# Order of ScalarE and VectorE work in the first Strassen pair: S1 split amid pair two's scalings, unit a ahead of S4, t2 amid the weight sums, row squares at the end

## The chip, the cores and the metric

The kernel runs on one core of one Trainium2 chip. The metric is device time in microseconds, the median of several executions. One more execution is recorded by the hardware profiler; from it come the page and the trace. The engines are named as in the profile: PE is TensorE's matmul, PEld its weight load, DVE is VectorE, ACT is ScalarE, SP is SyncE (here it only starts loads and stores).

## The reference, cut to what matters

One layer: RMS norm, a projection of 1056 tokens from 1024 to 3072 channels, two mixers (a gated short convolution and a pooling), an output projection, a residual and a final RMS norm.

```python
def _rmsnorm(x, g):
    r = lax.rsqrt(jnp.mean(xf * xf, axis=-1, keepdims=True) + EPS)
    return (xf * r).astype(x.dtype) * g

proj = jnp.einsum('bsd,de->bse', h, w_in)               # h: normalised x
b_g, c_g, u, z_a, v, z_b = jnp.split(proj, ...)
cu = c_g * u                                            # conv input
y_a = b_g * conv3(cu) * jax.nn.silu(z_a)
pooled = causal_window_mean(v) - v                      # windows 2, 4, 8, 16
y_b = (pooled @ pool_w) * pool_scale * jax.nn.silu(z_b)
y = concat(y_a, y_b) @ w_out ;  out = _rmsnorm(x + y, final_g)
```

All data is float32. The kernel computes a product of float32 numbers with three passes of a shorter format: each operand is split into a high half (ScalarE copies it) and a low half (VectorE subtracts the copy from the source), and high x low, low x high and high x high are added up. The norm's weight is folded into the projection weights, and its factor per token is applied to the products afterwards.

## The kernel before, in words

The tokens stand in three column blocks of 352 (n0, n1, n2; TN = 352), the channels in eight blocks of 128. The 24 output tiles of the projection are computed in twelve pairs. Pair zero is a plain product that runs while x arrives. Every later pair p computes its two tiles over n0 and n1 with one step of a Strassen-Winograd scheme, and over n2 plainly.

- The token side of the scheme is made once: A11, A12, A22, A21 and S1 to S4, each split into halves. S1f, S2f, S3f and S4f are the unsplit sums.
- The weight side is made for each pair. load_w(p) starts a load of 1 MB on SP into the buffer "tw", gain_w(p) scales it by the norm's weight on ScalarE (eight operations, L210), make_t(p) takes sums of it on VectorE (step 0 is L218, step 1 is L220 and L221), and make_unit(p, "a") to "d" splits raw weights (a, b) or sums (c, d) into units. The high half is ScalarE's at L158, the low half VectorE's at L159. In the profile the units are wa, wb, wc, wd.
- block(bank, p, name, x, ...) issues twelve matmuls of one unit half against one token block (L245). The blocks of a pair run in this order: B11 into bank a, T2 into b, T1 into c, the plain n2 product l, B21 into a, T3 into b, the plain product r, T4 into b, B22 into c. Pair one has its own order: l, B11, r, B21, T2, T1, T3, (B11 of pair two), T4, B22.
- VectorE reads the banks on the way: t1 = b + s1 must be taken before T3 adds to b, t2 = b + s1 before T4 adds to b. s1 is ScalarE's copy of bank a after B11.

Beside the pairs the kernel gets the norm's factor. For rows 0 to 639 square_rows(t, xk) on ScalarE squares a tile of 128 rows and sums it (L256); its tiles xk are loaded into R, R2 and up, and load_rows refills R and R2 for tiles three and four after their first squares. For the rest of the tokens squares_last and squares_head make squares earlier, and sums_last and sums_head (VectorE, L267 to L285) add them into acc. In pair two, hook "rest" lets TensorE sum acc over channels (L292), ScalarE copies that out (L293, L294), and rows() makes the factor in a chain of small operations of both engines (L300 to L310) and two diagonal matrices (L314 on ScalarE, L315 on VectorE), which six matmuls pr (L322) spread over the partitions. The hook "early" of pair two then loads, scales and sums pair three's weights.

What sets the order: up to the end of pair one, PE, ACT, DVE and POOL keep the order in which the code is written (`tc.manual_schedule(engines={ET.PE, ET.Activation, ET.DVE, ET.Pool})`). From pair two on, only PE does; a scheduler orders the others by its own estimates. SP's loads start in order, each when its buffer is free. The last reader of pair two's raw weights is the low half of unit b of pair two (L159); then pair three's load can start.

Of the kernel before, what the change touches and what calls it, by code (L numbers as in the profile page):

```python
# [15 lines left out]
KD = D // P  # L16
KH = KD // 2
# [45 lines left out]
def trunk(ctx, tc, xt, xres, xct, w_first, w_in, w_out, pool_w, par, fg, sconv, spool,  # L63
# [13 lines left out]
    MUL, ADD, SUB = ALU.mult, ALU.add, ALU.subtract  # L77
    n0, n1, n2 = cols
    vt = nc.vector.tensor_tensor

    def tmp(name, dtype=F32):
        return tp.tile([P, TOK], dtype, tag="tmp", name=name)
# [7 lines left out]
    def xtile(tag, name):  # L90
        return xp.tile([P, 2, KH, TN], F32R, tag=tag, name=name)
# [26 lines left out]
    def load_w(p):  # L118
        t = wp.tile([P, 4, KH * P], F32, tag="tw", name=f"wraw_{p}")
        nc.sync.dma_start(t, w_in[:, 2 * p - 2:2 * p].rearrange("p t (h k) c -> p (t h) (k c)", h=2))  # L120
        wraw[p] = t
# [34 lines left out]
    def split2(hi, lo, src):  # L156

        nc.scalar.activation(hi, src, AF.Copy)  # L158
        nc.vector.tensor_tensor(lo, src, hi.bitcast(F32), op=ALU.subtract)  # L159

    def split(dst, src):
        split2(dst[:, 0], dst[:, 1], src)
# [7 lines left out]
    def split_x(n, k, m):  # L170
        dst = blocks[n, k // KH]
        ks = slice(k % KH, k % KH + m)
        split2(dst[:, 0, ks], dst[:, 1, ks], raw[n][:, k:k + m])


    def wtile(i, shape, name, dtype=F32R):
        return wp.tile(shape, dtype, tag=f"wt{i}", name=name)
# [3 lines left out]
    def prep_w0(k):  # L181
        t, q = w0[k // KH], k % KH
        src, g = wfraw[:, k, :2 * P], wfraw[:, k, 2 * P:]
        nc.scalar.activation(t[:, 0, q], src, AF.Copy, scale=g)
        nc.vector.scalar_tensor_tensor(t[:, 1, q], src, g, t[:, 0, q].bitcast(F32),
                                       op0=ALU.mult, op1=ALU.subtract)
# [3 lines left out]
    def project_first(n, k):  # L190
        if k == 0:
            for i in range(2):
                pm[i, n] = bank(f"pm_{i}_{n}")[:, :TN]
        for s, (a, b) in enumerate(((0, 0), (1, 0), (0, 1))):
            for i in range(2):
                nc.tensor.matmul(pm[i, n], w0[k // KH][:, a, k % KH, i * P:(i + 1) * P],  # L196
                                 blocks[n, k // KH][:, b, k % KH],
                                 start=k == 0 and s == 0, stop=k == KD - 1 and s == 2)
# [4 lines left out]
    unit = {}  # L203
    tw = {}

    def gain_w(p):
        for k in range(KD):
            t = wraw[p][:, 0::2] if k < KH else wraw[p][:, 1::2]
            t = t[:, :, k % KH * P:(k % KH + 1) * P]
            nc.scalar.activation(t, t, AF.Copy, scale=gain[:, k:k + 1])  # L210

    def make_t(p, steps=(0, 1)):
        w = wraw[p]
        if 0 in steps:
            tw[p] = wp.tile([P, 4, KH * P], F32, tag="wraw", name=f"tw_{p}")
        t = tw[p]
        if 0 in steps:
            vt(t[:, 0:2], w[:, 2:4], w[:, 0::2], op=SUB)  # L218
        if 1 in steps:
            vt(t[:, 2], w[:, 3], t[:, 0], op=SUB)  # L220
            vt(t[:, 3], w[:, 1], t[:, 2], op=SUB)  # L221
# [3 lines left out]
    def make_unit(p, u):  # L225
        if p not in slot:

            q = slot[p - 1]
            slot[p] = {"a": q["spare"], "d": q["a"], "c": q["c"], "b": q["d"], "spare": q["b"]}
        t = wtile(slot[p][u], [P, 2, 2, KH * P], f"w{u}_{p}")  # L230
        src = {"a": wraw, "b": wraw, "c": tw, "d": tw}[u][p][:, 0:2 if u in "ac" else 4][:, -2:]
        split(t, src)
        unit[p, u] = t
# [17 lines left out]
    def load_rows(t, xk):  # L251
        nc.sync.dma_start(xk, xres[t * P:(t + 1) * P])
        return xk

    def square_rows(t, xk):
        nc.scalar.activation(xk, xk, AF.Square, accum_out=ss[:, t:t + 1])  # L256
# [4 lines left out]
    def squares_head(acc):  # L261
        sh = vb[:, PM:PM + KD * REST].rearrange("p (k c) -> p k c", k=KD)
        nc.scalar.activation(sh, raw[1][:, :, TN - REST:], AF.Square)
        return sh
# [6 lines left out]
    def squares_last():  # L271
        sq = []
        for k in range(0, KD, 3):
            t = tmp(f"sq_{k}").rearrange("p (k c) -> p k c", c=TN)[:, :min(3, KD - k)]
            nc.scalar.activation(t, raw[2][:, k:min(k + 3, KD)], AF.Square)
            sq.append(t)
        return sq
# [231 lines left out]
    with tc.manual_schedule(engines={ET.PE, ET.Activation, ET.DVE, ET.Pool}):  # L509
        for k in range(KD):  # L510
            prep_w0(k)
            for n in (2, 0):
                split_x(n, k, 1)
                project_first(n, k)
        nc.vector.tensor_copy(gain.rearrange("p (k o) -> p k o", o=1), wfraw[:, :, 2 * P:])
        nc.sync.dma_start(part, par)
        xk = [load_rows(t, q[:, :D]) for t, q in enumerate((R, R2, up[:, 2:]))]
        slot[1] = {"a": 2, "b": 3, "d": 4, "c": 0}
        slot[2] = {"a": 1, "d": 2, "c": 0, "b": 4, "spare": 3}
        acc = tmp("acc")  # L520
        for k in range(0, KD, 2):
            split_x(1, k, 2)
        for k in range(KD):
            project_first(1, k)
        sh = squares_head(acc)

        S3f, S2f, S1f = raw[1][:, :KH], raw[1][:, KH:], raw[0][:, :KH]
        vt(S3f, raw[0][:, :KH], raw[1][:, :KH], op=SUB)
        vt(S2f, raw[1][:, KH:], S3f, op=SUB)
        vt(S1f, raw[0][:, :KH], S2f, op=ADD)  # L530
        gain_w(1)
        make_unit(1, "a")
        make_t(1)
        make_unit(1, "b")
        load_w(2)
        for n in (2, 0):
            for i in range(2):
                nc.scalar.copy(heads[i][:, cols[n]], pm[i, n])
        sq = squares_last()
        make_unit(1, "d")  # L540
        S4f = [tp.tile([P, 2, TN], F32, tag="tmp", name=f"S4f_{h}") for h in range(2)]
        for h in range(2):
            ks = slice(2 * h, 2 * h + 2)
            vt(S4f[h], raw[0][:, KH:][:, ks], S2f[:, ks], op=SUB)
        S2 = xtile("xa", "S2")
        split(S2, S2f)
        S3 = xtile("xb", "S3")
        split(S3, S3f)


        t_0, um = tmp("t_0"), up[:, 2:]

        def plain1(i):
            pt = bank(f"lr{i}_1")[:, :TN]
            block(pt, 1, ("B11", "B12")[i], pl[0], True, False)
            block(pt, 1, ("B21", "B22")[i], pl[1], False, True)
            return pt

        pL = plain1(0)
        pa, pb, pc = (bank(f"{q}_1")[:, :TN] for q in "abc")  # L560
        s1, t1, t2 = t_0[:, n1], um[:, n0], um[:, n1]
        block(pa, 1, "B11", A11, True, False)
        nc.scalar.copy(s1, pa)
        make_unit(1, "c")
        square_rows(2, xk[2])
        gain_w(2)
        S1 = xtile("xc", "S1")
        split(S1, S1f)
        pR = plain1(1)
        block(pa, 1, "B21", A12, False, True)  # L570
        block(pb, 1, "T2", S2, True, False)
        vt(t1, pb, s1, op=ADD)
        S4 = xtile("xd", "S4")
        for h in range(2):
            ks = slice(2 * h, 2 * h + 2)
            split2(S4[:, 0, ks], S4[:, 1, ks], S4f[h])
        make_unit(2, "a")
        make_t(2)
        for i in range(2):
            nc.scalar.copy(heads[i][:, n1], pm[i, 1])  # L580
        block(pc, 1, "T1", S1, True, False)
        nc.scalar.copy(t_0[:, n2], pL)
        nc.scalar.copy(t_0[:, n0], pa)
        for t in range(2):
            square_rows(t, xk[t])
        xk += [load_rows(t, xk[t - 3]) for t in (3, 4)]
        block(pb, 1, "T3", S3, False, False)
        vt(t2, pb, s1, op=ADD)  # L588
        make_unit(2, "d")
        vt(um[:, n1], pc, t2, op=ADD)  # L590
        first_a(2)
        block(pb, 1, "T4", A22, False, True)
        vt(t_0[:, n1], pb, s1, op=ADD)
        make_unit(2, "c")
        block(pc, 1, "B22", S4, False, True)
        vt(um[:, n0], pc, t1, op=ADD)
        for t in (3, 4):
            square_rows(t, xk[t])
        for _ in sums_last(acc, sq):
            pass  # L600
        sums_head(acc, sh)
        make_unit(2, "b")
        vt(up[:, 2 + 2 * TN:], pR, t_0[:, n2], op=MUL)
        vt(up[:, 2:2 + 2 * TN], um[:, both], t_0[:, both], op=MUL)
    diag = []
# [276 lines left out]
```

## Time and profile before

| | |
|---|---|
| median of three runs | 376.91 us (376.59 to 377.08) |
| the profiled execution's time | 376.85 us |
| its span, first to last instruction | 375.1 us |
| mean granted TensorE clock | 0.995 |
| ACT busy, share of the span | 178.6 us, 48% |
| pair one, TensorE's first T2 to pair two's l | 41.03 to 58.67 us |

A timeline row has the start in us, the length in us, the engine, the line, the operation, output <- inputs, partitions and elements, and how many instructions were merged; in brackets stands the idle time ahead of it and what ended that. The length of a merged row reaches to the end of its last instruction, so neighbours can overlap: the time from start to start is what an engine needs. A row of waits has the total in us, how often, and the longest. A row of loads ends with the size and the time from issue to landing.

### The profile page before, as it was taken

Reading aid. Unit: us, or ns where it says so; the run is one execution under the profiler, and the core shown is the slowest. Engines: PE = TensorE matmul, PEld = TensorE weight load, DVE = VectorE, ACT = ScalarE, POOL = GpSimd, SP = SyncE. Lnnn points to the kernel's source line nnn. Section 1 sums busy time; section 2 is a strip of 40 time slices with the busy share of each in tenths; the row PEclk is TensorE's granted clock in tenths of the full one; section 3 lists DMA queues with packets and bytes.
Section 4 is the critical chain, followed back from the end, with each engine's and each line's share of the span. In section 5 each row is a group of like instructions: output and inputs, shape, how many; then the busy total and the mean of one; then the engine's idle time right before and its main releaser. Section 6 shows DMA issues by size and latency. Waiting matters only on the chain.

```text
span 375.1 us, 5275 instructions
## 1 busy us (share of the span) xinstructions
PE 365.2 (97%) x2114; PEld 350.1 (93%) x2114; DVE 275.4 (73%) x425; ACT 178.6 (48%) x313; POOL 1.4 (0%) x7
## 2 busy tenths in 40 slices
PE   9999999999999999999999999999999999999993
PEld 6999889999989999999999999999988889999883
DVE  4799688699999787677798776887289537222593
ACT  5799881949453453626354451731088124111212
POOL 0000000000000000000000000000000000000000
PEclk9999999999999999999999999999999999999998
DMA  7973033021041305012030511305549904000042
GB/s 205 418 265 112 3 112 114 0 85 57 2 170 59 114 0 196 34 28 86 2 112 0 204 56 33 136 6 191 210 144 381 416 32 168 4 0 2 0 182 112
DMA packets 13512, 41.68 MB, mean 111 GB/s; under 512 B 3760, under 2 KB 5040, under 8 KB 12080
## 3 DMA queue, kind: packets, MB, share of 16 engines
q1 hardware_dynamic: 13344, 41.02, 29.8%
q8 instruction: 16, 0.26, 0.3%
q10 hardware_dynamic: 144, 0.33, 0.2%
q14 instruction: 8, 0.07, 0.1%
HBM read 32.92 MB, written 8.42 MB: 110 GB/s over the span
## 4 chain that ended last, share of the span: by engine, by line
PE 78%; DVE 12%; ACT 4%; issue 2%; DMA 2%; SPq 1%; DVEq 0%; ACTq 0%
PE po L712 15%; PE b L245 13%; PE pc L782 10%; PE c L245 9%; PE r L245 8%; PE l L245 8%; PE a L245 8%; PE pm L196 5%; ACT wraw L210 2%; DMA raw<-in_xt_dram 2%; PE pp L399 1%; PE lr L245 1%; DVE yc L416 1%; DVE tw L218 1%; DVE wa L159 1%
## 5 line engine op out<-in xcount | busy, mean ns | idle before, releaser
L712 PE MATMUL po<-wo,mix 128*128 128x512 f32 (+1 forms) x264 | 56.5, 374 | 0.0
L712 PEld LDWEIGHTS po<-wo,mix 128*128 128x128 f32 x264 | 46.2, 188 | 9.7 <-DVE mix L159 0.2
L245 PE MATMUL a<-A,wa 128*128 128x352 f32 x264 | 46.4, 324 | 0.0
L245 PEld LDWEIGHTS a<-A,wa 128*128 128x128 f32 x264 | 43.3, 188 | 0.0
L210 ACT ACTIVATE wraw<-wraw,gain 128x256 f32<-128x256 f32 x88 | 36.8, 499 | 10.0 <-DMA wraw<-in_w_in_dram 10.0
L245 PE MATMUL r<-pl,wb 128*128 128x352 f32 x240 | 40.4, 324 | 0.0
L245 PE MATMUL l<-pl,wa 128*128 128x352 f32 x240 | 40.4, 324 | 0.0
L245 PEld LDWEIGHTS l<-pl,wa 128*128 128x128 f32 x240 | 39.1, 188 | 0.0
L245 PEld LDWEIGHTS r<-pl,wb 128*128 128x128 f32 x240 | 39.1, 188 | 0.0
L782 PE MATMUL pc<-mix,wo 128*128 128x416 f32 x192 | 36.5, 351 | 0.0
L782 PEld LDWEIGHTS pc<-mix,wo 128*128 128x128 f32 x192 | 35.9, 188 | 0.5
L245 PE MATMUL c<-S,wc 128*128 128x352 f32 x132 | 23.2, 324 | 0.9 <-DVE S L159 0.9
L245 PE MATMUL b<-A,wd 128*128 128x352 f32 x132 | 23.3, 325 | 0.7 <-DVE up L588 0.7
L245 PE MATMUL b<-S,wc 128*128 128x352 f32 x132 | 23.2, 324 | 0.7 <-DVE t L459 0.7
L245 PE MATMUL b<-S,wd 128*128 128x352 f32 x132 | 23.5, 324 | 0.1
L245 PE MATMUL c<-S,wb 128*128 128x352 f32 x132 | 23.1, 324 | 0.0
L245 PEld LDWEIGHTS b<-A,wd 128*128 128x128 f32 x132 | 21.6, 188 | 1.3 <-DVE up L588 0.9
L245 PEld LDWEIGHTS c<-S,wc 128*128 128x128 f32 x132 | 21.6, 188 | 1.2 <-DVE S L159 1.2
L245 PEld LDWEIGHTS b<-S,wc 128*128 128x128 f32 x132 | 21.6, 188 | 1.0 <-DVE t L459 1.0
L245 PEld LDWEIGHTS b<-S,wd 128*128 128x128 f32 x132 | 21.7, 188 | 0.4 <-DVE wd L159 0.4
L245 PEld LDWEIGHTS c<-S,wb 128*128 128x128 f32 x132 | 21.7, 188 | 0.0
L218 DVE TENSOR_TENSOR tw<-wraw 128x1024 f32<-128x1024 f32 x11 | 13.5, 1226 | 10.5 <-ACT wraw L210 10.5
(197 smaller groups left out, 528.1 us busy)
## 6 DMA issues: line engine op xcount, KB each, us to landing
wraw<-in_w_in_dram SPq DMA_DIRECT2D x11, 1024.0 KB, 4.6
woraw<-in_w_out_dram SPq DMA_DIRECT2D x8, 512.0 KB, 5.7
zt<-in_xres_dram SPq DMA_DIRECT2D x5, 512.0 KB, 6.4
spill_b<-yb SPq DMA_DIRECT2D x4, 528.0 KB, 3.5
mixraw<-spill_b SPq DMA_DIRECT2D x4, 528.0 KB, 5.8
R<-in_xres_dram SPq DMA_DIRECT2D x4, 512.0 KB, 7.9
out_yt_dram<-zt SPq DMA_DIRECT2D x4, 512.0 KB, 2.6
zc<-in_xct_dram SPq DMA_DIRECT2D x4, 416.0 KB, 6.4
```

The lines of the kernel that those rows point to most:

```text
L159: nc.vector.tensor_tensor(lo, src, hi.bitcast(F32), op=ALU.subtract)
L196: nc.tensor.matmul(pm[i, n], w0[k // KH][:, a, k % KH, i * P:(i + 1) * P], blocks[n, k // KH][:, b, k % KH], start=k == 0 and s == 0, stop ...
L210: nc.scalar.activation(t, t, AF.Copy, scale=gain[:, k:k + 1])
L218: vt(t[:, 0:2], w[:, 2:4], w[:, 0::2], op=SUB)
L245: nc.tensor.matmul(pt, t[:, a, i, k * P:(k + 1) * P], x[:, b, k], start=first and s == 0, stop=last and s == len(seq) - 1, skip_group_chec ...
L399: nc.tensor.matmul(pt[:, :TN], pws[:, a, g, :], pooled[g][b][:, cols[n]], start=(s == 0), stop=(s == 2))
L416: nc.vector.scalar_tensor_tensor(yc[:, :SEQ], up[:, t:t + SEQ], cw[t], yc[:, :SEQ], op0=ALU.mult, op1=ALU.add)
L712: nc.tensor.matmul(pt, mix[k][:, b, t * P:(t + 1) * P], wo[k][:, a, c], start=(k == 0 and s == 0), stop=(k == KD - 1 and s == 2))
L782: nc.tensor.matmul(pt, wo[k][:, a, d * P:(d + 1) * P], mix[k][:, b, T0:], start=(k == 0 and s == 0), stop=(k == KD - 1 and s == 2))
```

## The change

In the part whose order is written by hand, pair one:

- gain_w takes a range of blocks. Pair two's eight scalings are cut in two fours, and the split of S1 stands between them.
- Unit a of pair two is made right behind the scalings, ahead of t1 and of the split of S4; the row square of tile two goes behind it.
- make_t(2) is cut in its two steps. Step 0 stays, step 1 goes behind t2; the sum um (n1) goes ahead of unit d.
- The row squares of tiles zero and one no longer stand together: tile zero's stays near its place, tile one's goes behind the end of the pair, and each load of a further tile stands behind its square.
- Unit b of pair two is made ahead of the last squares and of the sums for acc.

```diff
-    def gain_w(p):
-        for k in range(KD):
+    def gain_w(p, ks=range(KD)):
+        for k in ks:
...
         make_unit(1, "c")
-        square_rows(2, xk[2])
-        gain_w(2)
+        gain_w(2, range(0, KH))
         S1 = xtile("xc", "S1")
         split(S1, S1f)
+        gain_w(2, range(KH, KD))
+        make_unit(2, "a")
+        square_rows(2, xk[2])
         pR = plain1(1)
...
             split2(S4[:, 0, ks], S4[:, 1, ks], S4f[h])
-        make_unit(2, "a")
-        make_t(2)
+        make_t(2, (0,))
...
-        for t in range(2):
-            square_rows(t, xk[t])
-        xk += [load_rows(t, xk[t - 3]) for t in (3, 4)]
+        square_rows(0, xk[0])
+        xk.append(load_rows(3, xk[0]))
         block(pb, 1, "T3", S3, False, False)
         vt(t2, pb, s1, op=ADD)
+        make_t(2, (1,))
+        vt(um[:, n1], pc, t2, op=ADD)
         make_unit(2, "d")
-        vt(um[:, n1], pc, t2, op=ADD)
         first_a(2)
...
         vt(um[:, n0], pc, t1, op=ADD)
+        square_rows(1, xk[1])
+        xk.append(load_rows(4, xk[1]))
+        make_unit(2, "b")
         for t in (3, 4):
             square_rows(t, xk[t])
         for _ in sums_last(acc, sq):
             pass
         sums_head(acc, sh)
-        make_unit(2, "b")
```

ScalarE in pair one, before, from unit c of pair one on (wraw_386 is pair two's raw weights, S_465 is S1, S_518 is S4; L256 is a row square):

```order
L158 ACTIVATE wc_453<-tw_379 128x1024
L256 ACTIVATE up,ss<-up 128x1024
L210 ACTIVATE wraw_386<-wraw_386,gain 128x2x128 x8
L158 ACTIVATE S_465<-raw_89 128x1408
L158 ACTIVATE S_518<-S4f_401 128x704
L158 ACTIVATE S_518<-S4f_402 128x704
L158 ACTIVATE wa_523<-wraw_386 128x1024
```

The same place after (S_460 is S1, S_521 is S4):

```order
L158 ACTIVATE wc_453<-tw_379 128x1024
L210 ACTIVATE wraw_386<-wraw_386,gain 128x2x128 x4
L158 ACTIVATE S_460<-raw_89 128x1408
L210 ACTIVATE wraw_386<-wraw_386,gain 128x2x128 x4
L158 ACTIVATE wa_467<-wraw_386 128x1024
L256 ACTIVATE up,ss<-up 128x1024
L158 ACTIVATE S_521<-S4f_401 128x704
L158 ACTIVATE S_521<-S4f_402 128x704
```

S1's high half now stands behind four scalings instead of a square and eight, and S4's behind the rest, unit a's and the square.

VectorE in pair one, before, from S4's low halves on (wa, wd and wc are units of pair two, tw_526 its weight sums; L588 is t2):

```order
L159 TENSOR_TENSOR S_518<-S4f_402,S_518 128x704
L159 TENSOR_TENSOR wa_523<-wraw_386,wa_523 128x1024
L218 TENSOR_TENSOR tw_526<-wraw_386 128x1024
L220 TENSOR_TENSOR tw_526<-wraw_386,tw_526 128x512
L221 TENSOR_TENSOR tw_526<-wraw_386,tw_526 128x512
L588 TENSOR_TENSOR up<-b_438,t_411 128x352
L159 TENSOR_TENSOR wd_563<-tw_526,wd_563 128x1024
```

The same place after (L588 is still t2; L590 is the sum um over n1):

```order
L159 TENSOR_TENSOR S_521<-S4f_402,S_521 128x704
L218 TENSOR_TENSOR tw_526<-wraw_386 128x1024
L588 TENSOR_TENSOR up<-b_438,t_411 128x352
L220 TENSOR_TENSOR tw_526<-wraw_386,tw_526 128x512
L221 TENSOR_TENSOR tw_526<-wraw_386,tw_526 128x512
L590 TENSOR_TENSOR up<-c_439,up 128x352
L159 TENSOR_TENSOR wd_562<-tw_526,wd_562 128x1024
```

t2 moved ahead of two of the three weight sums, and the low half of unit a went ahead of S4's.

ScalarE around the row sums of pair two, where the scheduler decides, before (wb is unit b of pair two, wraw_749 pair three's raw weights, rest the sums from TensorE):

```order
L158 ACTIVATE wb_620<-wraw_386 128x1024
L293 COPY ss<-rest 128x3
L294 COPY ss<-rest 32x1
L301 ACTIVATE mru<-mru 128x9
L309 ACTIVATE rh<-mru 128x9
L314 ACTIVATE diag_702<-ident,rh 128x128 x8
L314 ACTIVATE diag_702<-ident,rh 128x32
L210 ACTIVATE wraw_749<-wraw_749,gain 128x2x128 x8
```

The same place after (the rows between wb and the first scaling are the two last row squares):

```order
L158 ACTIVATE wb_611<-wraw_386 128x1024
L256 ACTIVATE R,ss<-R 128x1024
L256 ACTIVATE R_137,ss<-R_137 128x1024
L210 ACTIVATE wraw_749<-wraw_749,gain 128x2x128
L293 COPY ss<-rest 128x3
L294 COPY ss<-rest 32x1
L210 ACTIVATE wraw_749<-wraw_749,gain 128x2x128
L301 ACTIVATE mru<-mru 128x9
L210 ACTIVATE wraw_749<-wraw_749,gain 128x2x128 x3
L309 ACTIVATE rh<-mru 128x9
L210 ACTIVATE wraw_749<-wraw_749,gain 128x2x128
L314 ACTIVATE diag_702<-ident,rh 128x128 x8
```

Six of pair three's eight scalings, which stood behind the diagonals, now stand ahead of them, one of them ahead of the copy of the row sums. VectorE's order from the row sums to the end of pair four is unchanged.

## The prediction

> **What bounds the kernel now.** I read the page first, then TensorE's waits, then its timeline by blocks, and last ScalarE, VectorE and the load queue around the gaps.
>
> ```profile
> PE 365.2 (97%) x2114; PEld 350.1 (93%) x2114; DVE 275.4 (73%) x425; ACT 178.6 (48%) x313; POOL 1.4 (0%) x7
> ```
> ```profile
> PE c L245 <- DVE S L159: 0.9, 1, 0.9
> ...
> PE b L245 <- DVE t L459: 0.7, 1, 0.7
> PE b L245 <- DVE up L588: 0.7, 1, 0.7
> ```
>
> TensorE is busy 97% of the span, so the program is bound by it, and only its gaps can be won or lost. Three waits in the middle name VectorE: for the low half of S1 (L159), for t2 (L588), for t1 of pair four (L459). The sizes are better read from starts in TensorE's timeline (start, us, line, tiles, count):
>
> ```profile
> 41.03 2.10 PE L245 MATMUL b<-S,wd 128*128 128x352 f32 x12
> 44.06 2.21 PE L245 MATMUL c<-S,wc 128*128 128x352 f32 x12 [0.93 <-DVE S L159]
> 46.11 2.10 PE L245 MATMUL b<-S,wc 128*128 128x352 f32 x12
> 48.05 2.10 PE L245 MATMUL a<-A,wa 128*128 128x352 f32 x12
> 50.81 2.21 PE L245 MATMUL b<-A,wd 128*128 128x352 f32 x12 [0.66 <-DVE up L588]
> ...
> 58.67 4.04 PE L245 MATMUL l<-pl,wa 128*128 128x352 f32 x24
> 62.55 0.88 PE L292 MATMUL rest<-one,acc 128*128 128x1 f32 x8
> ...
> 67.35 1.33 PE L322 MATMUL pr<-diag,onesr 128*128 128x352 f32 x6
> 68.52 4.05 PE L245 MATMUL r<-pl,wb 128*128 128x352 f32 x24
> ...
> 78.23 2.45 PE L245 MATMUL b<-S,wd 128*128 128x352 f32 x12
> ...
> 94.33 2.21 PE L245 MATMUL b<-A,wd 128*128 128x352 f32 x12
> ...
> 109.47 2.10 PE L245 MATMUL a<-A,wa 128*128 128x352 f32 x12
> 112.31 2.21 PE L245 MATMUL b<-S,wc 128*128 128x352 f32 x12 [0.74 <-DVE t L459]
> 114.36 4.04 PE L245 MATMUL r<-pl,wb 128*128 128x352 f32 x24
> ```
>
> Twelve matmuls take 1.94 us from start to start (46.11 to 48.05), one 0.162. From 41.03 to 58.67 TensorE issues 96 of them, eight blocks: 15.52 us of work in 17.64, so **2.12 us are lost in pair one**. From 68.52 to 114.36 stand 273: 44.13 of work in 45.84, so **1.70 are lost in pairs two to four**: 0.35 in the block at 78.23 (2.45 long, not 2.10), 1.0 around 112.31 (0.90 late after 109.47, then 2.05 to the next start), the rest, 0.35, around 94.33.
>
> The wait rows say less: 0.93 and 0.66, that is 1.6, for pair one. The Trainium skill (Perfetto Trace Analysis, "Per-instruction lifecycle", Tensor Engine Instruction) says that a matmul's reported end is computed from its size and not observed. The trace agrees: after a wait a block takes 2.05 to the next start (44.06 to 46.11) where its neighbours take 1.94. By the wait rows alone (0.93, 0.66, 0.74, less the 0.32 found below) the gain would be 2.0 us and the time 374.8; I take the starts.
>
> **The change, part by part.** Pair one on ScalarE and VectorE before (columns as above):
>
> ```profile
> 35.76 1.07 ACT L158 ACTIVATE wc<-tw 128x1024 fp32r<-128x1024 f32 x1
> 36.73 1.05 ACT L256 ACTIVATE up<-up 128x1024 f32<-128x1024 f32 x1
> ...
> 37.77 3.31 ACT L210 ACTIVATE wraw<-wraw,gain 128x256 f32<-128x256 f32 x8
> 40.97 1.38 ACT L158 ACTIVATE S<-raw 128x1408 fp32r<-128x1408 f32 x1
> 44.04 1.48 ACT L158 ACTIVATE S<-S4f 128x704 fp32r<-128x704 f32 x2 [1.69 <-DVE S L159]
> ```
> ```profile
> 42.38 1.63 DVE L159 TENSOR_TENSOR S<-raw,S 128x1408 fp32r<-128x1408 f32 x1 [3.01 <-ACT S L158]
> ...
> 44.87 1.69 DVE L159 TENSOR_TENSOR S<-S4f,S 128x704 fp32r<-128x704 f32 x2 [0.43 <-ACT S L158]
> ...
> 47.65 1.22 DVE L218 TENSOR_TENSOR tw<-wraw 128x1024 f32<-128x1024 f32 x1
> ...
> 49.63 0.69 DVE L221 TENSOR_TENSOR tw<-wraw,tw 128x512 f32<-128x512 f32 x1
> 50.24 0.52 DVE L588 TENSOR_TENSOR up<-b,t 128x352 f32<-128x352 f32 x1
> ...
> 55.91 1.25 DVE L281 TENSOR_TENSOR sq<-sq,sq 128x1056 f32<-128x1056 f32 x1
> ...
> 60.21 0.22 DVE L269 TENSOR_TENSOR acc<-vb 128x64 f32<-128x64 f32 x1
> ```
> ```profile
> 32.37 0.35 SPq L120 DMA_DIRECT2D wraw<-in_w_in_dram  x1
> ...
> 61.60 19.82 SPq L120 DMA_DIRECT2D wraw<-in_w_in_dram  x2
> ```
> ```profile
> wraw<-in_w_in_dram SPq DMA_DIRECT2D x3, 1024.0 KB, 4.6
> ...
> up<-in_xres_dram SPq DMA_DIRECT2D x1, 512.0 KB, 11.6
> ```
>
> *S1 amid the scalings.* Eight scalings take 3.20 (37.77 to 40.97), one 0.40. Pair two's weights land at 32.37 + 4.6 = 36.97, so four scalings now run from 37.0 to 38.6, S1's high half to 39.98 (1.38), its low half to 41.64 (1.63). TensorE is ready for T1 at 41.03 + 1.94 = 42.97, so the first wait goes with 1.3 us to spare.
>
> *Unit a, then S4.* ScalarE: four scalings to 41.5, a's high half (1.07) to 42.55, the row square (1.05) to 43.5, S4's halves (1.48) to 45.0. VectorE: a's low half to 43.8, t1 (0.52) to 44.25, S4's low halves (1.69) to 46.0, first weight sum (1.22) to 47.2. Behind t1 queues T3, which adds to the bank that t1 reads: T3 is due at 44.91, 0.65 later. So the work put ahead of t1 costs nothing.
>
> *t2 amid the weight sums.* T3 ends at 44.91 + 2.10 = 47.0; t2 now follows the first sum and is done at 47.65. TensorE reaches T4 at 44.91 + 2 x 1.94 = 48.79 (the a block between needs a's low half of 43.8), so the second wait goes with 1.1 to spare. Together the whole **2.12**.
>
> *What is late next.* The sum's second step comes behind t2 (two operations, 1.4): 49.0. Unit d's halves follow (1.07 and 1.22): 51.3. TensorE wants d at 41.03 + 6 x 1.94 = 52.67. Unit c's low half, behind d and one 0.5 addition that waits for T4, ends near 52.9; wanted at 54.61. Both covered, by 1.35 and 1.7.
>
> *Row squares and their loads.* No work is added, three squares of 1.05 move. The loads of rows three and four queue behind their own squares on SP: the first issues at about 47.3, the second at about 52.3. The last square ends near 58; its reader comes after 61. Free, with 3 us of cover.
>
> *Unit b ahead of the sums.* b's low half ends near 54.6. The sums follow, 55.91 to 60.43 before (4.52), now 54.5 to 59.0; TensorE asks for them at 62.55 - 2.12 = 60.43. Free by 1.4. But b's low half is the last reader of pair two's raw weights, and the load into that buffer was issued at 61.60, right behind it; now at 54.6, and 4.6 later, at 59.2, pair three's weights are there.
>
> The rows of that stage, ScalarE and then VectorE:
>
> ```profile
> 63.47 0.16 ACT L293 COPY ss<-rest 128x3 f32<-128x3 f32 x1 [6.75 <-PE rest L292]
> ...
> 63.91 0.21 ACT L301 ACTIVATE mru<-mru 128x9 f32<-128x9 f32 x1 [0.24 <-DVE mru L300]
> ...
> 65.52 2.68 ACT L314 ACTIVATE diag<-ident,rh 128x128 fp32r<-128x128 f32 x9
> 68.11 3.31 ACT L210 ACTIVATE wraw<-wraw,gain 128x256 f32<-128x256 f32 x8
> ```
> ```profile
> 71.44 1.23 DVE L218 TENSOR_TENSOR tw<-wraw 128x1024 f32<-128x1024 f32 x1 [2.81 <-ACT wraw L210]
> ...
> 111.72 0.54 DVE L459 TENSOR_TENSOR t<-b,s 128x352 f32<-128x352 f32 x1
> ```
>
> *Six scalings in the gaps of the row chain.* ScalarE's order now has one scaling ahead of the copy at L293, one ahead of the Sqrt (L301), three ahead of rh, one ahead of the diagonals. The first is over at 59.7, 1.6 before the copy's new 61.35. The second (0.40) fills a gap of about 0.3 and delays the Sqrt by some 0.1; three (1.2) and the sixth (0.40) stand in the 1.6 between the Sqrt and the diagonals (63.91 to 65.52), where rh's own 0.2 lies too: 0.2 over. Sum 0.32. All of it reaches TensorE, whose six pr matmuls (67.35) take 1.17 to the next block instead of 0.97: they already end on the diagonals. Bounds: 0, or six scalings one after the other, 2.4. I take 0.32, since the gaps in the rows hold nearly all. So r of pair two starts at 68.52 - 2.12 + 0.32 = 66.72, **1.80** earlier.
>
> *VectorE's long stretch.* It works without a break from 71.44 to 111.72, and its start hung on the eighth scaling. With two scalings left behind the diagonals (which end at 66.4) it starts at 67.15, 4.3 earlier, while TensorE is 1.8 earlier: 2.5 us of new lead. It may now wait for TensorE here and there; with a few tenths lost so, the lead is still twice the largest loss there (1.0), and the **1.70** go too. After 114.36 TensorE has no wait to win.
>
> Sum: 2.12 - 0.32 + 1.70 = 3.50. Against the profiled execution's 376.85 (span 375.1; 0.06 under the median of 376.91) this gives **373.35**, called 373.4.
>
> **The rivals.**
> A: VectorE's lead doesn't come, and the 1.70 remain: 376.85 - 1.80 = 375.05. For it: the stretch is full, so any late start is paid in full. Against: the load has 2 us of cover. It decides if the first sum of pair three starts after 68.6 in part, after 69.6 in whole.
> B: the six scalings run as a block in the row chain: 2.1 more than I took, on TensorE as on VectorE: 375.4. It needs the weights to land around 61; for it speaks that the order allows it.
> C, the other side: the scaling ahead of L293 holds the row sums because the weights land late, and ScalarE can't pass it. Each us after 61.0 costs one on TensorE. At 64.5 all gain is gone, and from 65.2, 10.6 us after the issue, the program is slower; with 11.6, which the row load at the start took in the crowd of first loads, the scaling ends at 66.6, 5.25 after the copy's time: 378.6. Against: three such weight loads took 4.6, and only one row load is near.
> D: the waits of pair one move to the next block, T2 of pair two waiting for unit d: with d 2.1 late, at 54.8, pair one's gain is gone (375.5), with 3.5, at 56.2, all of it (376.9). That is 4.9 behind my count.
>
> **How the numbers follow.** Forecast 0.68, A 0.12, B 0.10, D 0.06, C 0.04. The measurement tells 0.2% (0.75 us) from no change. Forecast, A and B are faster: 0.90; D the same: 0.06; C slower: 0.04. Range: down to 372.8 (no 0.32, and the runs' own 0.25 below their median), up to 375.4 (A and B).
>
> **What would show it.** After: no wait at T1 or T4 of pair one, l of pair two at 56.55; pair three's load issued near 54.6; r of pair two near 66.7, pair three's first sum near 67.2; no wait of TensorE on t1 of pair four, its r at 110.9. A wait of L293 on a scaling shows C; a wait at T2 of pair two, D; a pr stage well over 1.5, towards 3.5, B. Wrong would be, first of all, a low half or a load that takes longer in its new company than in these rows.

## The result and the profile after

| | before | after |
|---|---|---|
| median | 377.0 us (376.59 to 377.1, 4 runs) | 373.53 us (373.06 to 373.68, 4 runs) |
| ratio | | 0.9909, 95% interval 0.9897 to 0.9922 |
| profiled execution, its span | 376.85, 375.1 us | 373.68, 371.9 us |
| TensorE busy | 365.2 us, 97% | 363.6 us, 98% |

The kernel is 3.5 us, or 0.9%, faster. TensorE's waits in the profile after:

```profile
PE warm L97 <- PEq L878: 0.8, 1, 0.8
PE pm L196 <- ACT pl L158: 0.8, 1, 0.8
PE pm L196 <- ACT A L158: 0.2, 1, 0.2
PE pr L322 <- ACT diag L314: 0.2, 1, 0.2
```

The three waits on VectorE (S1, t2, t1 of pair four) are gone. The first three lines belong to the first 12.3 us, the start of the program and the arrival of x; the last is the wait for the diagonals. TensorE's timeline after (start, us, tiles, count):

```profile
41.45 2.10 PE L245 MATMUL b<-S,wd 128*128 128x352 f32 x12
43.39 2.10 PE L245 MATMUL c<-S,wc 128*128 128x352 f32 x12
...
49.21 2.10 PE L245 MATMUL b<-A,wd 128*128 128x352 f32 x12
...
56.97 4.04 PE L245 MATMUL l<-pl,wa 128*128 128x352 f32 x24
60.85 0.88 PE L292 MATMUL rest<-one,acc 128*128 128x1 f32 x8
...
65.64 0.96 PE L322 MATMUL pr<-diag,onesr 128*128 128x352 f32 x5
66.78 0.43 PE L322 MATMUL pr<-diag,onesr 128*128 128x352 f32 x1 [0.18 <-ACT diag L314]
67.06 4.04 PE L245 MATMUL r<-pl,wb 128*128 128x352 f32 x24
...
76.76 2.10 PE L245 MATMUL b<-S,wd 128*128 128x352 f32 x12
...
92.28 2.10 PE L245 MATMUL b<-A,wd 128*128 128x352 f32 x12
...
109.24 2.10 PE L245 MATMUL b<-S,wc 128*128 128x352 f32 x12
111.19 4.05 PE L245 MATMUL r<-pl,wb 128*128 128x352 f32 x24
```

T1 follows T2 after 1.94, T4 stands where the blocks put it, and from l of pair two to r of pair four one gap is left, at pr. TensorE came to its first T2 at 41.45 and not 41.03. This is the start-up alone: the 0.42 is there when its block at 13 us starts (13.38 after, 12.95 before), and from there both need 28.1 to T2. So stages are compared by differences of starts, us, from one trace of each kernel:

| kernel | first T2 | T2 to l of pair two | l to r | r to r of pair four | T2 to r of pair four |
|---|---|---|---|---|---|
| before | 41.03 | 17.64 | 9.85 | 45.84 | 73.33 |
| after | 41.45 | 15.52 | 10.09 | 44.13 | 69.74 |
| after_again | 41.07 | 15.52 | 10.09 | 44.13 | 69.74 |
| b_back | 41.72 | 15.52 | 9.83 | 45.82 | 71.17 |
| b_alone | 40.55 | 17.63 | 10.09 | 44.14 | 71.86 |
| t2_back | 41.07 | 16.08 | 10.09 | 44.12 | 70.29 |
| s1_back | 40.87 | 16.02 | 10.08 | 44.13 | 70.23 |
| free_back | 41.01 | 15.52 | 10.09 | 44.14 | 69.75 |
| row_plus | 40.71 | 15.52 | 11.12 | 44.12 | 70.76 |
| full_r | 41.53 | 15.52 | 9.64* | 44.13* | 69.29 |
| half_r | 41.29 | 15.52 | 9.65* | 44.13* | 69.30 |
| half_r_again | 41.08 | 15.52 | 9.64* | 44.13* | 69.29 |

(* r stands elsewhere there: the stage is l to T4 less r's 3.88, and the next one is T4 to r of pair four and 3.88.)

The change took 2.12 in pair one, gave 0.24 back at the row chain and took 1.71 in pairs two to four: 3.59. The span fell by 3.2, as the start-up was 0.42 later; from r of pair four to the end both need 260.7. The rows behind it, ScalarE after:

```profile
37.74 1.71 ACT L210 ACTIVATE wraw<-wraw,gain 128x256 f32<-128x256 f32 x4 [0.49 <-DMA wraw<-in_w_in_dram]
39.35 1.36 ACT L158 ACTIVATE S<-raw 128x1408 fp32r<-128x1408 f32 x1
40.62 1.70 ACT L210 ACTIVATE wraw<-wraw,gain 128x256 f32<-128x256 f32 x4
...
60.34 0.51 ACT L210 ACTIVATE wraw<-wraw,gain 128x256 f32<-128x256 f32 x1 [2.74 <-DMA wraw<-in_w_in_dram]
61.76 0.16 ACT L293 COPY ss<-rest 128x3 f32<-128x3 f32 x1 [0.91 <-PE rest L292]
...
62.28 0.19 ACT L301 ACTIVATE mru<-mru 128x9 f32<-128x9 f32 x1
62.38 1.29 ACT L210 ACTIVATE wraw<-wraw,gain 128x256 f32<-128x256 f32 x3
63.58 0.20 ACT L309 ACTIVATE rh<-mru 128x9 fp32r<-128x9 f32 x1
63.68 0.49 ACT L210 ACTIVATE wraw<-wraw,gain 128x256 f32<-128x256 f32 x1
64.08 2.65 ACT L314 ACTIVATE diag<-ident,rh 128x128 fp32r<-128x128 f32 x9
```

S1 stands between two fours of scalings, and the scalings of pair three fill the row chain's gaps: from L293 to the diagonals it takes 2.32 where it took 2.05. VectorE after:

```profile
40.75 1.63 DVE L159 TENSOR_TENSOR S<-raw,S 128x1408 fp32r<-128x1408 f32 x1 [0.93 <-ACT S L158]
...
47.91 0.52 DVE L588 TENSOR_TENSOR up<-b,t 128x352 f32<-128x352 f32 x1
...
67.56 1.23 DVE L218 TENSOR_TENSOR tw<-wraw 128x1024 f32<-128x1024 f32 x1 [0.64 <-ACT wraw L210]
...
96.46 1.23 DVE L159 TENSOR_TENSOR wd<-tw,wd 128x1024 fp32r<-128x1024 f32 x1 [0.40 <-ACT wd L158]
...
108.54 0.52 DVE L459 TENSOR_TENSOR t<-b,s 128x352 f32<-128x352 f32 x1
```

S1's low half is ready at 42.38, t2 at 48.43, and t1 of pair four at 109.06, before T3 at 109.24: by only 0.18.

### The profile page after: what moved, and what is told of

Read it like the earlier page. It is cut to its first block, busy times and chain, and to the rows that moved or that the text cites. A ratio compares the mean times of both kernels' runs of the same rounds, so it can differ in the third digit from the quotient of the medians.

```text
span 371.9 us, 5275 instructions
## 1 busy us (share of the span) xinstructions
PE 363.6 (98%) x2114; PEld 349.3 (94%) x2114; DVE 275.3 (74%) x425; ACT 177.8 (48%) x313; POOL 1.4 (0%) x7
## 4 chain that ended last, share of the span: by engine, by line
PE 94%; DMA 2%; ACT 2%; SPq 1%; DVE 0%; issue 0%; DVEq 0%
PE b L245 17%; PE po L715 15%; PE c L245 11%; PE a L245 11%; PE r L245 10%; PE l L245 10%; PE pc L785 10%; PE pm L196 5%; PE lr L245 2%; DMA raw<-in_xt_dram 2%; PE pp L399 2%; ACT diag L314 1%; SPq L106 1%; SPq L110 0%; ACT wraw L210 0%
## 5 line engine op out<-in xcount | busy, mean ns | idle before, releaser
L158 ACT ACTIVATE wb<-wraw 128x1024 fp32r<-128x1024 f32 x11 | 11.6, 1059 | 17.9 <-PE b L245 17.9
```

## The experiments

By their medians b_back and b_alone stand clear of the changed kernel: their intervals lie wholly above its 0.9897 to 0.9922. The intervals of all other runs overlap it, so their sizes are read from the stages of one trace each.

**b_back.** The changed kernel, unit b of pair two behind the sums again:

```diff
-        make_unit(2, "b")
         for t in (3, 4):
...
         sums_head(acc, sh)
+        make_unit(2, "b")
```

> The changed kernel with one edit undone: unit b of pair two is made behind the sums for acc again. Theory (two separate gains: 2.1 us in pair one from S1 and t2, and 1.5 us net in pairs two to four, which hangs on unit b's early end, because that lets pair three's weights load early): pair three's load is issued only near 60, no scaling stands ahead of the diagonals, TensorE's waits at 78, 94 and 112 come back, time 377.0 - 2.1 = 374.9. Rival (VectorE's stretch gains because pair one's two waits are gone, b's place is worth nothing): 373.5.

Measured 374.5 us, ratio to before 0.9943 (0.9929 to 0.9958). This is 0.4 under the expectation. The six runs lie between 374.42 and 376.07, and the profiled one took 375.4; its first T2, at 41.72, is the latest of all traces. By the stages the edit costs 1.43. Pair one keeps its 15.52; all of pairs two to four's loss is back, 45.82. SP's load, ScalarE, VectorE and TensorE's wait in this kernel:

```profile
60.04 0.33 SPq L120 DMA_DIRECT2D wraw<-in_w_in_dram  x1
```
```profile
64.09 2.66 ACT L314 ACTIVATE diag<-ident,rh 128x128 fp32r<-128x128 f32 x9
66.66 3.29 ACT L210 ACTIVATE wraw<-wraw,gain 128x256 f32<-128x256 f32 x8
```
```profile
69.98 1.23 DVE L218 TENSOR_TENSOR tw<-wraw 128x1024 f32<-128x1024 f32 x1 [2.78 <-ACT wraw L210]
```
```profile
PE b L245 <- DVE t L459: 0.7, 1, 0.7
```

Pair three's load starts at 60.04 (55.42 after), its first sum at 69.98 (67.56), and TensorE waits for t1 of pair four again. The rival falls: without b's early end the shorter pair one doesn't help the later pairs.

The load's late landing isn't itself what holds the first sum back here. It lands 4.5 after its issue, at 64.5, and ScalarE runs the scalings without a wait right behind the diagonals, all eight. What differs is their place: from the first T2 the first sum is 28.26 away here and 26.11 in the changed kernel, 2.15 less, and six scalings of 0.40 less the 0.24 of the row chain are 2.16. The early load is what allows this place: the changed kernel's first scaling runs at 60.34, and weights whose load starts at 60.04 are not there by then. That the scheduler moved the scalings because of it follows from no run by itself.

**b_alone.** The kernel before with that edit alone (the same line, moved the other way).

> The kernel before with that one edit alone: unit b of pair two ahead of the last squares and sums. Theory: pair one keeps its waits on S1 and t2 (2.1 us), pair three's load is issued near 57 instead of 61.6, seven scalings fit ahead of the diagonals and cost TensorE 0.2 to 0.4 there, the 1.7 us of pairs two to four go: 377.0 - 1.4 = 375.6. Rival (b's place worth nothing alone): 377.0.

Measured 375.4 us, 0.9960 (0.9947 to 0.9973). Pair one keeps its loss (17.63), pairs two to four lose nothing (44.14), the row chain costs 0.24 more. The load starts at 56.66, seven scalings stand ahead of the diagonals, and the first sum comes 27.83 after the first T2 where it took 30.41 before: 2.58 less, and seven scalings less 0.24 are 2.56. Both parts add up: 73.33 falls by 2.16 with b_back, by 1.47 with b_alone, together 3.63; with both it falls by 3.59.

**t2_back.** The changed kernel, t2 behind both steps of the weight sums:

```diff
-        make_t(2, (0,))
+        make_t(2)
...
         vt(t2, pb, s1, op=ADD)
-        make_t(2, (1,))
```

> The changed kernel with t2 behind both steps of pair two's weight sums again. Theory: t2 ends near 49.85 where TensorE wants T4 at 49.2, a wait of 0.65 and 0.1 of slower restart, which nothing gives back later: 373.5 + 0.75 = 374.25. Rival (the wait is absorbed at the row sums, where TensorE waits for the diagonals anyway): 373.5.

Measured 373.93 us, 0.9919 (0.9906 to 0.9931); pair one is 0.56 longer, and the stages behind it are as after. TensorE's and VectorE's rows of it:

```profile
49.27 2.21 PE L245 MATMUL b<-A,wd 128*128 128x352 f32 x12 [0.28 <-DVE up L588]
51.32 2.10 PE L245 MATMUL c<-S,wb 128*128 128x352 f32 x12
```
```profile
48.70 0.52 DVE L588 TENSOR_TENSOR up<-b,t 128x352 f32<-128x352 f32 x1
```

T4 was due at 46.89 + 1.94 = 48.83 and starts 0.44 later, and its block takes 2.05 to the next start. Nothing gives this back: from r of pair four to the end it takes 260.7 too. The size is 0.2 under the expectation, which was worked out from after's own trace: there pair two's scalings began 3.71 ahead of the first T2 (37.74), here 3.99 (37.08), since the weights had landed sooner.

**s1_back.** The changed kernel, S1 behind all eight scalings:

```diff
-        gain_w(2, range(0, KH))
+        gain_w(2)
         S1 = xtile("xc", "S1")
         split(S1, S1f)
-        gain_w(2, range(KH, KD))
```

> The changed kernel with S1's split behind all eight scalings again (the row square stays behind unit a). Theory: S1's low half ends near 44.0 where TensorE wants T1 at 43.4, a wait of 0.6 and 0.1 of restart: 373.5 + 0.7 = 374.2. Rival (absorbed later): 373.5. Between before and this, the square alone would then have been worth 0.4.

Measured 373.78 us, 0.9914 (0.9901 to 0.9927); pair one is 0.50 longer, the wait for S1 is back (TensorE, then ScalarE):

```profile
43.20 2.21 PE L245 MATMUL c<-S,wc 128*128 128x352 f32 x12 [0.22 <-DVE S L159]
```
```profile
36.91 3.31 ACT L210 ACTIVATE wraw<-wraw,gain 128x256 f32<-128x256 f32 x8 [0.24 <-DMA wraw<-in_w_in_dram]
```

T1 was due at 40.87 + 1.94 = 42.81 and starts 0.39 later, and its block takes 0.11 more to the next start. The 0.50 is 0.2 under the expectation, and as in t2_back the scalings began sooner ahead of the first T2: 3.96, not 3.71. Before, S1 cost 1.2 (1.09 of wait, 0.11 of restart). So four scalings ahead of S1 instead of eight are worth 0.5. The 0.7 between is, by difference, the place of tile two's row square: before, the scalings stood behind it and began 3.26 ahead of the first T2, here they wait only for the weights and begin 0.70 sooner. The expectation said 0.4. No run moves that square by itself.

**free_back.** The changed kernel with most of the moves undone that the prediction costed at nothing. Two stay: the square of tile two goes ahead of unit a and S4 again, but remains behind S1, and the sum um (n1) remains ahead of unit d:

```diff
-        make_unit(2, "a")
         square_rows(2, xk[2])
...
+        make_unit(2, "a")
         make_t(2, (0,))
...
-        square_rows(0, xk[0])
-        xk.append(load_rows(3, xk[0]))
+        for t in range(2):
+            square_rows(t, xk[t])
+        xk += [load_rows(t, xk[t - 3]) for t in (3, 4)]
...
-        square_rows(1, xk[1])
-        xk.append(load_rows(4, xk[1]))
```

> The changed kernel with the moves undone that were costed at nothing: unit a of pair two behind S4 again, row square two ahead of S4, squares zero and one together again ahead of t2. S1 amid the scalings, t2 amid the sums and unit b's early place stay. Theory: no wait of TensorE comes back (a's low half ends near 47.0 where its block starts at 47.3, t2 near 48.6 where T4 starts at 49.2), 373.5. Rival (the changed order of a and of the squares carries part of pair one's 2.1): 0.3 to 1.0 more.

Measured 373.09 us, 0.9901 (0.9886 to 0.9916); every stage is that of after within 0.01. The moves undone here are worth nothing beside the others.

**row_plus.** Five multiplications by 1.0, one behind the other, in rows():

```diff
         nc.vector.tensor_tensor(r, r, u, op=ALU.mult)
+        for _ in range(5):
+            nc.vector.tensor_scalar(r, r, 1.0, None, op0=ALU.mult)
```

> The changed kernel with five more multiplications by 1.0 in the row chain, one behind the other, 0.2 each: the chain is 1.0 longer, no result changes. Theory (the chain from the row sums to the diagonals holds TensorE one to one): the stage from l of pair two to r grows from 10.1 to 10.9 (1.0 more, less 0.2 of scalings that now fit the longer gap), TensorE's waits in pairs three and four stay away, 373.5 + 0.8 = 374.3. Rival (other work hides it): 373.5.

Measured 373.94 us, 0.9930 (0.9917 to 0.9942). The stage from l to r grows by 1.03, one to one with the 1.00 that the five operations take in the trace, and the later pairs lose nothing. (The median is 0.4 over after's but 0.85 over free_back's, which ran on the same chip.) The 0.2 that was to come off did not: the scheduler put seven scalings into the longer chain, and one still stands ahead of the diagonals (ScalarE):

```profile
61.64 2.09 ACT L210 ACTIVATE wraw<-wraw,gain 128x256 f32<-128x256 f32 x5
63.86 0.21 ACT L311 ACTIVATE rh<-mru 128x9 fp32r<-128x9 f32 x1
63.98 0.49 ACT L210 ACTIVATE wraw<-wraw,gain 128x256 f32<-128x256 f32 x1
64.38 2.65 ACT L316 ACTIVATE diag<-ident,rh 128x128 fp32r<-128x128 f32 x9
```

**full_r and half_r.** Since TensorE waits for the row chain, work that needs no rows can stand ahead of pr: all of the product r (full_r), or its first twelve matmuls (half_r). In half_r:

```diff
         hooks["early"]()
-        hooks.get("rows", lambda: None)()
-        pR = plain(1, f"r_{p}")
+        pR = bank(f"r_{p}")[:, :TN]
+        block(pR, p, "B12", pl[0], True, False)
+        hooks.get("rows", lambda: None)()
+        block(pR, p, "B22", pl[1], False, True)
```

> The changed kernel with TensorE's order in pair two changed: the plain product r (24 matmuls, 3.9) ahead of the six pr matmuls, not behind. Theory: TensorE no longer waits for the diagonals, the stage from l to the block behind r and pr loses 0.45 (10.1 to 9.65 with pr's place swapped), the norm's rows reach VectorE 3.4 later, at about 70.4, just when it asks for them, 373.5 - 0.45 = 373.1. Rival (VectorE's lead over TensorE at t1 of pair four, 0.2 in the changed kernel's trace, is used up): a wait at pair four's T3 of up to 1.0 and 374.

> The same with half of r (12 matmuls, 1.9) ahead of the pr matmuls. Theory: as full_r for TensorE (pr is reached 1.9 later, the diagonals are ready 1.1 after its old start), and the rows reach VectorE only 1.5 later: 373.1. Rival: 373.5 or more, with a wait at pair four's T3.

Measured 373.0 us, 0.9898 (0.9884 to 0.9911), and 372.91 us, 0.9897 (0.9883 to 0.9910). Both win 0.45 by the trace, and no wait comes at pair four. TensorE in half_r:

```profile
65.48 2.11 PE L245 MATMUL r<-pl,wb 128*128 128x352 f32 x12
67.43 1.13 PE L322 MATMUL pr<-diag,onesr 128*128 128x352 f32 x6
68.39 2.11 PE L245 MATMUL r<-pl,wb 128*128 128x352 f32 x12
70.34 2.10 PE L245 MATMUL b<-A,wd 128*128 128x352 f32 x12
```

The six pr matmuls take 0.96 to the next start, without a wait. VectorE's lead isn't used up: t1 of pair four is ready 0.2 ahead of T3 in both, as in after. Its scheduled order changed as well, and unit a's low half now stands ahead of the first use of the rows; no run shows whether the lead holds for that reason.

**after_again and half_r_again**, on one chip:

> The changed kernel once more, beside half_r on the same chip. 373.5; from the first T2 to r of pair four 69.7 in its trace whatever the start-up of the run, which moved TensorE's first T2 between 40.5 and 41.7 in the runs so far.

> The kernel with half of r ahead of the pr matmuls once more, beside the changed kernel. Theory (0.45 won at the diagonals and kept): 373.1, from the first T2 to r of pair four 69.3. Rival (the 0.45 is lost in the run's start-up scatter or given back behind pair four): the same time as the changed kernel.

Measured 373.37 us, 0.9901 (0.9886 to 0.9915), and 373.04 us, 0.9898 (0.9880 to 0.9915). In their traces the way from the first T2 to r of pair four is 69.74 and 69.29. The traces show the 0.45; the times, 0.33 apart with overlapping intervals, don't settle it. By the traces half_r and full_r, alike within 0.01, are the best of the versions tried.

## Why the prediction was right

- *S1 and t2: 2.12.* Measured 2.12 (17.64 to 15.52). s1_back and t2_back bring the two waits back singly, with 0.50 and 0.56, half of the whole. Of the rest 0.70 is, by difference, the move of tile two's square behind S1. The prediction uses it without naming it: its scalings run from 37.0, while the square ended at 37.78 before, and it lists the squares as free. The last 0.36 no run tells apart. The covers were 0.3 to 0.4 smaller than forecast, 1.0 at S1 and 0.8 at t2, since the scalings began 3.71 ahead of the first T2 and not 4.0: the load took 4.8 to land, not 4.6.
- *Starts, not wait rows.* By the wait rows the gain would have been 2.0. The traces show 3.59. In t2_back the wait row says 0.28, the starts say 0.44, and with the slower restart the block costs 0.56. The Trainium skill (Perfetto Trace Analysis, "Per-instruction lifecycle") says that a matmul's end is estimated from the size of the instruction and a memory delay, not observed. The trace agrees: in an unbroken row a block is 2.10 long though the next starts after 1.94, and these 0.16 are what the wait row lacks.
- *Unit b and the load.* The outcome held: b_back and b_alone show that b's early end starts pair three's load early, lets six or seven scalings stand ahead of the diagonals and wins pairs two to four. The times in it were 0.4 too early: load at 55.42 for 54.6 (0.42 of it start-up), its landing 4.8 after the issue, not 4.6. The scaling ahead of L293 was over 0.9 before the copy, not 1.6. So rival C was nearer than was said.
- *Row chain: 0.32.* Measured 0.24; row_plus shows that what the chain loses, TensorE loses.
- *VectorE's lead.* The first sum came 3.88 earlier on the clock of the trace and 4.30 with the start-up taken off, as forecast, and r 1.88 against 1.80. But the cover claimed for t1 of pair four, twice the largest loss of 1.0, was misjudged. The losses add up: before, t1 was ready at 112.26 where T3 was due at 111.41, 0.85 late, and TensorE had lost 0.70 of its 1.70 ahead of that already, so 1.55 of lead over TensorE was needed. Of the 4.30, 3.60 were left at t1 (111.72 to 108.54, with the start-up), and less TensorE's own 1.88 that is 1.72: 0.17 to spare, as the margin of 0.18 says. A part of what was lost on the way is the 0.40 at 96.46, where VectorE waits for unit d's high half: ScalarE's order has unit b's ahead of it, which waits 1.53 for TensorE. "A few tenths lost" was too little, 0.7 was. What took the rest is not traced. That the gain came whole was, by this small margin, luck.
- *The rivals.* A, B and D show none of their signs: the first sum is at 67.14 with the start-up taken off, the pr stage takes 1.42, and T2 of pair two doesn't wait. L293 waits for TensorE's sums (0.91) and not for a scaling, so C stayed away too.
- *The sum.* 3.50 forecast, 3.59 by the traces, 3.47 by the medians.

## What to carry to other kernels

Where one engine is nearly full, count its work from start to start in each stage; what is left over is all that reordering can win, and the one forecast here was right to 0.1. Ask of a moved step not only who reads its result but whose buffer it frees: the early split of unit b was worth 1.5. It let a load start 4 us sooner and the work on its data go ahead of the diagonals, while no wait of TensorE named that load. Where waits pile up along a stretch, compare a lead with their sum and not with the largest of them. Small operations put into the gaps of a chain cost what they overrun (0.24 here), and if the full engine has independent work, that work belongs ahead of the chain's end.

## What the runs showed of the hardware

With the same work of TensorE up to there, its first T2 started between 40.55 and 41.72 us in the twelve traces. The difference arises in the first 13 us, while the first pieces of x and of the weights arrive; from the block that TensorE starts at 12.5 to 13.6 us to the first T2 all twelve take 28.07 to 28.09. The waits named there, 0.2 to 1.3 on ScalarE's first splits, explain it only in part: with 0.2 named, T2 came at 40.71 in row_plus and at 41.08 in half_r_again. This scatter of a microsecond is larger than most single edits here, while the stages behind it that an edit leaves alone repeat within 0.02 from trace to trace.
